# One streaming-encoder layer: another order of the column blocks in the input projection, and one subtraction moved from GpSimd to VectorE

## The chip, the cores and the metric

The kernel runs on one core of a Trainium2 chip. The metric is the device time of one execution in microseconds (us). A core has a matrix engine (TensorE, PE in the profile, with its weight loads as PEld), VectorE (DVE), ScalarE (ACT), GpSimd (POOL) and SyncE (SP); each runs its own queue of instructions in order, and semaphores tie the queues together. SP, POOL and ACT also issue DMA transfers.

## The reference

The layer takes x (2048 tokens of 1024 channels) and 256 memory tokens, all in 32-bit floats. It has three parts: token mixing, cross attention into the memory, and a SwiGLU feed-forward with 2816 channels, each between two RMS norms and added to its input. The change lies in the mixing, which starts with one projection into 2816 columns:

```
u = rms_norm(h, g_mix_pre[l])
z = u @ w_in[l]
qa, ka, va, qh, fh, ih, gh = jnp.split(z, IN_SPLITS, axis=-1)
ya = swa_with_sinks(qa, ka, va, sinks[l])          # sliding-window attention
yh = hgrn2(qh, fh, ih, gh, lb, hgrn_onorm[l])      # gated linear recurrence, 4 heads of 128
y = jnp.concatenate([ya, yh], axis=-1) @ w_out[l]
```

In the recurrence the forget columns become decays. They are summed in chunks of 64 tokens, and the value in the middle of each chunk is subtracted before the exponentials:

```
qf = silu(q) * Dk ** -0.5
f = lb + (1 - lb) * sigmoid(f_logit); kf = 1 - f
b = cumsum(log(f)) within the chunk; b_mid = b[CHUNK // 2 - 1]
A = (qf * exp(b - b_mid)) @ (kf * exp(b_mid - b)).T
```

## The kernel before

**Numbers.** Every operand of a large product is split into a rounded high part and the rest (the low part), and each product is three matmuls, high by high, high by low and low by high (L1098, L1099, L1100). Splitting costs one pass for the high part, on ACT (L962) or POOL (L964), and one DVE pass for the low part (L965).

**Columns.** The 2816 columns of the input projection are 22 columns of 128: 0 to 5 for the attention, 6 to 9 the recurrence's queries, 10 to 13 its forget values, 14 to 17 its inputs i, 18 to 21 its gates g. The projection is computed transposed (columns on partitions, tokens along the free dimension), for the first 1024 tokens and then for the second 1024. The list `ORDER` (L427) gives eleven pairs of columns:

```
    ORDER = [(4, 5), (0, 1), (2, 3)] + [(10 + h, 6 + h) for h in range(4)] + [(c, c + 1) for c in range(14, 22, 2)]
```

**First half** (`in_first`, to about 240 us). Each pair is a block of 256 columns by 1024 tokens. The three attention blocks are computed plainly; the other eight go by a scheme with seven products in place of eight: the weights come in two raw tiles (`sraw`), some are added or subtracted on DVE (`sum`, L1067), each is split (`S`), and each product is 12 matmuls of 128x512 into one of the PSUM banks `psm`. ACT copies finished products away as addends (`part`, L1113), and DVE adds them to a later product (L602) into the block's result tile, `pair`. That last step empties the accumulator, so TensorE's next product in that bank waits for it. Then an activation follows: tanh on ACT (L608) and a scaling on POOL (L610) for a forget column, tanh (L614) and a DVE product (L615) for a query or a gate, nothing for i. TensorE computes the products of block after block; the blocks' follow-up work is emitted between the steps of the next block.

**Decays.** A forget column is followed by `decays` (L695 to L726): logarithm on ACT (L703), which needs the table of its function loaded first, two scans of 128x512 on DVE (L707, printed in the order as SCALAR_TENSOR_TENSOR), a copy of the middle values on POOL (L711, 128x16), the subtraction of the middle value from all 128x1024 (L712), small sums on POOL (L713, L716, L720), two exponentials on ACT (L721, L723) and a DVE pass (L726). Afterwards the query column of the same pair is multiplied by the exponential on DVE (L638).

**Second half.** `in_proj` goes through the same `ORDER` column by column, as 48 matmuls for each 512 tokens, between the steps of the sliding-window attention and the recurrence of the first half, and then between those of the second half's attention. There `decays` gets its two tiles from the pools `x` (three buffers) and `u`. In the second attention loop the same `x` tiles also hold pieces of the output weights `w_out`, which are added and subtracted and stored as `w_s` for a later product of the seven-product kind.

**Order.** A Python program emits all instructions in one stream. A scheduler then moves instructions within each engine's queue by estimated times, with the dependences and the buffers of the pools kept. So a change of `ORDER` moves instructions on every engine.

Of the kernel before, what the change touches and what calls it, by code (L numbers as in the profile page):

```python
# [11 lines left out]
F32 = mybir.dt.float32  # L12
# [3 lines left out]
ALU = mybir.AluOpType  # L16
AX = mybir.AxisListType

P = 128
T = 2048  # L20
D = 1024
# [12 lines left out]
C_KA, C_VA, C_QH, C_FH, C_IH, C_GH = 512, 640, 768, 1280, 1792, 2304  # L34
# [14 lines left out]
class Layer:  # L49
# [374 lines left out]
        self.W = ph.tile([P, 4, P], F32, tag="W", name="W0", bufs=3)  # L424
        nc.gpsimd.memset(self.W, 0.0)

    ORDER = [(4, 5), (0, 1), (2, 3)] + [(10 + h, 6 + h) for h in range(4)] + [(c, c + 1) for c in range(14, 22, 2)]  # L427

    def pair_tile(self):
        self._n += 1  # L430
        return self.st_pool.tile([P, 2, D], F32, tag="pair", name=f"pair_{self._n}", bufs=6)

    def normed(self, x, junk):
        nc = self.nc
        ss = self.small("n_s")
        nc.scalar.activation(junk, x, AF.Square, accum_out=ss)
        r = self.rstd([ss], D, "n")
        nc.vector.scalar_tensor_tensor(x, x, r, self.g_mix, ALU.mult, ALU.mult)

    def in_first(self):  # L440
# [13 lines left out]
        def x_load(q, s):  # L454
            for k in range(4):
                self.load(raw[q, s][:, k, :], I["x_t"][2 * s + q, :, k, :])
# [74 lines left out]
        def parted():  # L531
            for n in (1, 3, 2, 0):
# [5 lines left out]
                with self.behind() if n else contextlib.nullcontext():  # L538
# [7 lines left out]
                  + self.in_block(*p, beside[i], get if i > 6 else (), None if i else lambda: x_load(0, 0))  # L546
                  for i, p in enumerate(self.ORDER)]

# [22 lines left out]
    def in_block(self, ca, cb, beside, get, between):  # L571

        nc, w = self.nc, self.I["w_in"]
        z, bare = [], []

        def load(t, j):
            for i, c in enumerate((ca, cb)):
                if between and i and not j:
                    between()
                self.load(t[:, i, :], w[c, :, j * 512:(j + 1) * 512])  # L580

        def stream(kind):
            for _ in range(2):
                next(iter(get), None)
            return self.streamed(load, 4, kind, tiled=True)

        def out(i, j, a, b):
            if not z:
                z.append(self.pair_tile())
                bare.append(self.r_half is None)  # L590
            c0 = (ca, cb)[i] * P
            sl = slice(j * 512, (j + 1) * 512)
            zs = z[0][:, i, sl]
            if bare[0]:
                nc.scalar.activation(zs, a, AF.Copy)
                return
            if b is None:
                if ca < 6:
                    nc.vector.tensor_tensor(zs, a, self.r_half[:, sl], ALU.mult)
                    return  # L600
            else:
                nc.vector.tensor_tensor(zs, a, b, ALU.add)  # L602
                a = zs
            if C_IH <= c0 < C_GH:
                if b is None:
                    nc.scalar.activation(zs, a, AF.Copy)
            elif C_FH <= c0 < C_IH:
                nc.scalar.activation(zs, a, AF.Tanh, scale=0.5)  # L608
                h = (c0 - C_FH) // P
                nc.gpsimd.tensor_scalar(zs, zs, self.fb[:, h:h + 1], self.fa[:, h:h + 1], ALU.mult, ALU.add)  # L610
            else:
                self._n += 1
                t = self.st_pool.tile([P, 512], F32, tag="part", name=f"th_{self._n}", bufs=self.parts)
                nc.scalar.activation(t, a, AF.Tanh, scale=0.5)  # L614
                nc.vector.scalar_tensor_tensor(zs, t, 1.0, a, ALU.add, ALU.mult)  # L615

        def after():
            def rows(n):
                self._n += 1
                t = self.st_pool.tile([P, D], F32, tag="xr", name=f"xr_{self._n}", bufs=1)  # L620
                with self.behind():
                    self.load(t, self.I["x"][TB + n * P:TB + (n + 1) * P, :])
                return t

            while self.r_bc is None:
                yield
            if bare[0]:
                for i in range(2):
                    with self.behind():
                        nc.gpsimd.tensor_tensor(z[0][:, i, :], z[0][:, i, :], self.r_bc, ALU.mult)  # L630
            t = rows(beside[0]) if beside else None
            c0 = ca * P
            if C_FH <= c0 < C_IH:
                e = self.pair_tile()
                yield from self.decays(0, (c0 - C_FH) // P, z[0][:, 0, :], e[:, 0, :], e[:, 1, :])
                for j in range(2):
                    sl = slice(j * 512, (j + 1) * 512)
                    nc.vector.scalar_tensor_tensor(z[0][:, 1, sl], z[0][:, 1, sl], -0.5 * float(P) ** -0.5,  # L638
                                                   e[:, 0, sl], ALU.mult, ALU.mult)
            for i, c in enumerate((ca, cb)):  # L640
                (self.store if c < 18 else self.store_late)(self.z_d[c * P:(c + 1) * P, 0:TB], z[0][:, i, :])
            for _ in range(1 if C_FH <= c0 < C_IH else 3):
                yield
            for n in beside:
                if n != beside[0]:
                    t = rows(n)
                    for _ in range(3):
                        yield
                ss = self.small("n_s")
                with self.behind():  # L650
                    nc.scalar.activation(t, t, AF.Square, accum_out=ss)
                self.rstd([ss], D, "n", self.r_u[:, NPB + n:NPB + n + 1])
                yield

        return stream, out, after, None

    def in_proj(self, b, u):
        order = [c for p in self.ORDER for c in p]
        e1 = None
        for cols in [order[:2]] + [[c] for c in order[2:]]:  # L660
            e1 = self.in_cols(b, u, cols, e1)
            yield
# [35 lines left out]
    def decays(self, b, h, f, e1, e2):  # L698

        nc = self.nc  # L700
        NCB = TB // 64
        yield
        nc.scalar.activation(e1, f, AF.Ln)  # L703
        yield
        for s in range(TB // 512):
            sl = slice(s * 512, (s + 1) * 512)
            nc.vector.tensor_tensor_scan(e2[:, sl], self.reset.rearrange("p a b -> p (a b)"), e1[:, sl], 0.0,  # L707
                                         ALU.mult, ALU.add)
        b16 = e2.rearrange("p (c t) -> p c t", t=64)
        mid = self.small("d_mid", NCB)  # L710
        nc.gpsimd.tensor_scalar(mid, b16[:, :, 31], 1.0, 1.0, ALU.mult, ALU.mult)  # L711
        nc.gpsimd.tensor_tensor(b16, b16, mid.unsqueeze(2).broadcast_to([P, NCB, 64]), ALU.subtract)  # L712
        nc.gpsimd.tensor_scalar(self.dl[:, h, b * NCB + 1:(b + 1) * NCB + 1], b16[:, :, 63], 1.0, 1.0,  # L713
                                ALU.mult, ALU.mult)
        gs = self.small("d_g", NCB)
        nc.gpsimd.tensor_tensor(gs, mid, self.dl[:, h, b * NCB:(b + 1) * NCB], ALU.add)  # L716
        yield
        g2 = gs.rearrange("p (n c) -> p n c", c=2)
        nc.scalar.activation(self.G1[:, b * NPB:(b + 1) * NPB, h], g2[:, :, 1], AF.Exp)
        nc.gpsimd.tensor_tensor(g2[:, :, 1], g2[:, :, 0], g2[:, :, 1], ALU.add)  # L720
        nc.scalar.activation(e1, e2, AF.Exp)  # L721
        yield
        nc.scalar.activation(e2, e2, AF.Exp, scale=-1.0)  # L723
        nc.scalar.activation(self.G[:, b * NPB:(b + 1) * NPB, h, :], g2, AF.Exp)
        yield
        nc.vector.scalar_tensor_tensor(f, f, 1.0, e2, ALU.subtract, ALU.mult)  # L726
# [1035 lines left out]
```

## Time and profile before

| | before |
|---|---|
| median of 3 runs | 2573.41 us (2573.24 to 2574.53) |
| the profiled execution, its own time | 2571.13 us |
| its span in the trace | 2569.4 us |
| mean granted TensorE clock | 0.995 |
| first half's input projection | to about 240 us |
| second half's projection, with attention and recurrence | about 240 to 740 us |
| cross attention and feed-forward | the rest |

The profile shows one execution; an instruction's row has its start and its duration, and in brackets how long its engine had been idle before it and what ended that idle time. The granted clock is the share of full speed at which TensorE was allowed to run. The times of the stages are read from the lines that run in them.

### The profile page before, as it was taken

What the parts mean: (1) busy time and instruction counts of PE and PEld (TensorE: products, weight loads), DVE (VectorE), ACT (ScalarE), POOL (GpSimd) and SP (SyncE); (2) the same over time, 40 slices, a digit from 0 to 9 for tenths busy, and PEclk for the clock granted to TensorE, in tenths of its full rate; (3) what the DMA queues carried; (4) which work ended last, traced back from release to release, by engine and by line L of the source; (5) the groups of instructions that cost most, each with busy time, mean ns of one, the idle gap of its engine ahead of it and who ended that gap; (6) DMA issues with size and microseconds to landing.
All of it is one profiled execution on the core that took longest, in us unless ns stands there. A gap on an engine that the chain in (4) does not pass through costs nothing.

```text
span 2569.4 us, 34131 instructions
## 1 busy us (share of the span) xinstructions
PE 2517.3 (98%) x12012; PEld 2095.3 (82%) x12012; DVE 1751.8 (68%) x2801; ACT 1254.1 (49%) x2614; POOL 459.4 (18%) x637
## 2 busy tenths in 40 slices
PE   8999999999999999999999999999999999999998
PEld 7777888878997888888788888888888888888886
DVE  6876578877666578697785655575666566664756
ACT  5553366655554565565564333353333334543443
POOL 2341344320322233224210000000000000000022
PEclk9999999999999999999999999999999999999999
DMA  6262645484896896777983542253555434576798
GB/s 238 91 221 100 192 152 171 131 257 157 278 316 226 230 281 206 254 235 198 311 274 121 169 165 77 82 197 124 180 201 192 159 128 142 191 221 185 224 224 210
DMA packets 277835, 495.22 MB, mean 193 GB/s; under 512 B 20897, under 2 KB 135585, under 8 KB 277153
## 3 DMA queue, kind: packets, MB, share of 16 engines
q1 hardware_dynamic: 264128, 443.76, 51.7%
q0 software_dynamic: 11232, 40.90, 8.3%
q10 hardware_dynamic: 2304, 8.39, 0.8%
q8 instruction: 94, 1.54, 0.2%
q14 instruction: 77, 0.62, 0.1%
HBM read 330.45 MB, written 162.53 MB: 192 GB/s over the span
## 4 chain that ended last, share of the span: by engine, by line
PE 81%; DMA 7%; DVE 5%; issue 3%; POOL 2%; ACT 2%; SPq 0%; DVEq 0%; POOLq 0%; ACTq 0%
PE psm L1098 23%; PE psm L1100 22%; PE psm L1099 22%; PE psg L170 2%; PE psg L172 2%; PE psg L171 2%; PE pss L1351 1%; DVE S L965 1%; DMA qd<-z_d 1%; DMA row<-h_d 1%; DMA row<-d_s 1%; DMA kk<-z_d 1%; DMA row<-in_x_dram 1%; DVE T L965 1%; PE pss L811 0%
## 5 line engine op out<-in xcount | busy, mean ns | idle before, releaser
L1098 PE MATMUL psm<-T,S 128*128 128x512 f32 x2744 | 1063.1, 392 | 11.1 <-ACT S L962 4.5
L1100 PE MATMUL psm<-T,S 128*128 128x512 f32 x2744 | 1065.6, 391 | 8.0 <-DVE S L965 7.8
L1099 PE MATMUL psm<-T,S 128*128 128x512 f32 x2744 | 1071.6, 391 | 0.0
L1098 PEld LDWEIGHTS psm<-T,S 128*128 128x128 f32 x2744 | 516.4, 188 | 123.1 <-ACT S L962 6.5
L1100 PEld LDWEIGHTS psm<-T,S 128*128 128x128 f32 x2744 | 516.3, 188 | 120.0 <-DVE S L965 12.2
L1099 PEld LDWEIGHTS psm<-T,S 128*128 128x128 f32 x2744 | 516.4, 188 | 106.4
L962 ACT ACTIVATE S<-sum 128x512 fp32r<-128x512 f32 (+1 forms) x336 | 206.3, 618 | 328.6 <-PE psm L1100 321.8
L965 DVE TENSOR_TENSOR S<-sraw,S 128x512 fp32r<-128x512 f32 (+1 forms) x312 | 213.0, 690 | 214.5 <-ACT S L962 200.1
L965 DVE TENSOR_TENSOR S<-sum,S 128x512 fp32r<-128x512 f32 (+1 forms) x400 | 275.9, 694 | 77.7 <-ACT S L962 59.8
L1113 ACT ACTIVATE part<-psm 128x512 f32<-128x512 f32 x294 | 172.9, 591 | 182.6 <-PE psm L1100 177.3
L962 ACT ACTIVATE S<-sraw 128x512 fp32r<-128x512 f32 (+1 forms) x271 | 165.7, 617 | 159.6 <-PE psm L1100 149.6
L1469 POOL DMA_DIRECT2D row<-y_d x28 | 25.0, 894 | 1072.0 <-DMA sraw<-hid_d 905.3
L1440 ACT ACTIVATE junk<-row 128x512 f32<-128x512 f32 x160 | 99.6, 624 | 100.3 <-DVE row L1462 35.7
L170 PE MATMUL psg<-u,whi 128*128 128x512 f32 x352 | 143.8, 409 | 1.8 <-POOL whi L152 1.8
L965 DVE TENSOR_TENSOR T<-row,T 128x1024 fp32r<-128x1024 f32 x104 | 124.2, 1201 | 30.4 <-ACT T L962 30.2
L172 PE MATMUL psg<-u,wlo 128*128 128x512 f32 x352 | 142.2, 404 | 0.5 <-DVE wlo L153 0.5
L171 PE MATMUL psg<-u,whi 128*128 128x512 f32 x352 | 142.5, 405 | 0.0
L962 ACT ACTIVATE T<-row 128x1024 fp32r<-128x1024 f32 x104 | 105.3, 1023 | 21.9 <-DMA row<-in_w_down_dram 9.4
L1644 DVE TENSOR_TENSOR part<-psm,part 128x512 f32<-128x512 f32 x66 | 45.4, 688 | 65.0 <-PE psm L1100 64.9
L964 POOL TENSOR_SCALAR S<-sum 128x512 fp32r<-128x512 f32 x64 | 48.6, 765 | 218.2 <-PE psm L1100 158.0
L153 DVE TENSOR_TENSOR wlo<-raw,whi 128x1024 fp32r<-128x1024 f32 x54 | 69.3, 1283 | 23.1 <-ACT whi L150 18.4
L1635 DVE TENSOR_TENSOR row<-psm,part 128x512 f32<-128x512 f32 x66 | 45.4, 688 | 55.2 <-PE psm L1100 55.1
(329 smaller groups left out, 3461.2 us busy)
## 6 DMA issues: line engine op xcount, KB each, us to landing
sraw<-in_w_gate_dram SPq DMA_DIRECT2D x44, 512.0 KB, 5.1
sraw<-in_w_up_dram SPq DMA_DIRECT2D x44, 512.0 KB, 4.9
hid_d<-row SPq DMA_DIRECT2D x44, 512.0 KB, 2.7
h_d<-row SPq DMA_DIRECT2D x32, 512.0 KB, 7.0
y_d<-row SPq DMA_DIRECT2D x32, 512.0 KB, 4.0
sraw<-hid_d SPq DMA_DIRECT2D x32, 512.0 KB, 5.4
row<-h_d POOLq DMA_DIRECT2D x30, 512.0 KB, 7.7
row<-y_d POOLq DMA_DIRECT2D x28, 512.0 KB, 7.6
```

Source lines behind the costliest of these rows:

```text
L153: nc.vector.tensor_tensor(lo, raw, f32(hi), ALU.subtract)
L170: nc.tensor.matmul(ps, ah, bh, start=(i == 0), stop=False)
L171: nc.tensor.matmul(ps, ah, bl, start=False, stop=False)
L172: nc.tensor.matmul(ps, al, bh, start=False, stop=(i == n - 1))
L962: self.nc.scalar.activation(hi, raw, AF.Copy)
L964: self.nc.gpsimd.tensor_scalar(hi, raw, 1.0, 1.0, ALU.mult, ALU.mult)
L965: self.nc.vector.tensor_tensor(lo, raw, f32(hi), ALU.subtract)
L1098: nc.tensor.matmul(ps, s[:, 0, k, :], t[:, 0, k, :], start=st, stop=False, **kw)
L1099: nc.tensor.matmul(ps, s[:, 0, k, :], t[:, 1, k, :], start=False, stop=False, **kw)
L1100: nc.tensor.matmul(ps, s[:, 1, k, :], t[:, 0, k, :], start=False, stop=sp, **kw)
L1113: nc.scalar.activation(t, ps, AF.Copy)
L1440: self.nc.scalar.activation(junk, a, AF.Square, scale=float(D) ** -0.5, accum_out=to)
```

## The change

Two things. First, `ORDER` now puts a pair of i or gate columns behind each pair with a forget column, where before the four pairs with forget columns stood in a row: (10, 6), (14, 15), (11, 7), (16, 17), (12, 8), (18, 19), (13, 9), (20, 21). The second half follows the same list. Secondly, the subtraction of the middle value runs on DVE in the first half and stays on POOL in the second. Beside that, the last forget column of the first half gets one of the `g` tiles and the single `xr` tile in place of a `pair` tile for its logarithms and sums.

```
-    ORDER = [(4, 5), (0, 1), (2, 3)] + [(10 + h, 6 + h) for h in range(4)] + [(c, c + 1) for c in range(14, 22, 2)]
+    ORDER = [(4, 5), (0, 1), (2, 3)] + [p for h in range(4) for p in ((10 + h, 6 + h), (14 + 2 * h, 15 + 2 * h))]
...
+    def xr_tile(self):
+        self._n += 1
+        return self.st_pool.tile([P, D], F32, tag="xr", name=f"xr_{self._n}", bufs=1)
...
             if C_FH <= c0 < C_IH:
-                e = self.pair_tile()
-                yield from self.decays(0, (c0 - C_FH) // P, z[0][:, 0, :], e[:, 0, :], e[:, 1, :])
+                h = (c0 - C_FH) // P
+                if h < 3:
+                    e = self.pair_tile()
+                    e1, e2 = e[:, 0, :], e[:, 1, :]
+                else:
+                    e1, e2 = self.gain_tile(), self.xr_tile()
+                yield from self.decays(0, h, z[0][:, 0, :], e1, e2)
...
-        nc.gpsimd.tensor_tensor(b16, b16, mid.unsqueeze(2).broadcast_to([P, NCB, 64]), ALU.subtract)
+        (nc.gpsimd if b else nc.vector).tensor_tensor(b16, b16, mid.unsqueeze(2).broadcast_to([P, NCB, 64]),
+                                                      ALU.subtract)
```

Lines move down in the changed kernel: L602 is L606, L707 is L715, L712 is L720, L721 is L730, L726 is L735, L965 is L974, L1067 is L1076.

The queue of DVE at the decays of column 10, the first forget column, at about 112 us. `pair_853` holds its logarithms and sums, `pair_752` is the result tile of block (10, 6), `pair_914` that of the next block (its row L602 or L606 is an eviction), `S` are split weights and `sum` their combinations. Before:

```order
L965 TENSOR_TENSOR S_940<-sraw_664,S_940 128x512
L707 SCALAR_TENSOR_TENSOR pair_853<-reset,pair_853 128x512 x2
L602 TENSOR_TENSOR pair_914<-psm_945,part_844 128x512
L965 TENSOR_TENSOR S_961<-sraw_825,S_961 128x512
L638 SCALAR_TENSOR_TENSOR pair_752<-pair_752,pair_853 128x512 x2
L965 TENSOR_TENSOR S_986<-sum_984,S_986 128x512
L602 TENSOR_TENSOR pair_914<-psm_854,part_887 128x512
L726 SCALAR_TENSOR_TENSOR pair_752<-pair_752,pair_853 128x1024
```

After:

```order
L974 TENSOR_TENSOR S_935<-sraw_664,S_935 128x512
L715 SCALAR_TENSOR_TENSOR pair_853<-reset,pair_853 128x512 x2
L606 TENSOR_TENSOR pair_914<-psm_940,part_844 128x512
L974 TENSOR_TENSOR S_954<-sraw_825,S_954 128x512
L720 TENSOR_TENSOR pair_853<-pair_853,d_mid_896 128x1024
L974 TENSOR_TENSOR S_977<-sum_975,S_977 128x512
L1076 TENSOR_TENSOR sum_1051<-sraw_825 128x512
L646 SCALAR_TENSOR_TENSOR pair_752<-pair_752,pair_853 128x512 x2
L606 TENSOR_TENSOR pair_914<-psm_854,part_887 128x512
L735 SCALAR_TENSOR_TENSOR pair_752<-pair_752,pair_853 128x1024
```

Behind the scans follow an eviction and a split (`S_961`, now `S_954`) as before. Then the subtraction (L720) comes in, and the product of the query (L638, now L646), which stood ahead of the next split (`S_986`, now `S_977`), stands behind it and a sum. `pair_914` is block (11, 7) before and block (14, 15) after.

The same queue at the decays of column 11, from the scans on. Before, from about 122 us, where `pair_1024` holds the sums and `pair_914` is block (11, 7), and L615 is the query's product:

```order
L707 SCALAR_TENSOR_TENSOR pair_1024<-reset,pair_1024 128x512 x2
L602 TENSOR_TENSOR pair_914<-psm_831,part_867 128x512
L965 TENSOR_TENSOR S_1042<-sum_1040,S_1042 128x512
L965 TENSOR_TENSOR S_1062<-sum_1060,S_1062 128x512
L1067 TENSOR_TENSOR sum_1160<-sraw_994,sraw_997 128x512
L615 SCALAR_TENSOR_TENSOR pair_914<-th_937,pair_914 128x512
L1067 TENSOR_TENSOR sum_1195<-sum_1160,sraw_994 128x512
L965 TENSOR_TENSOR S_1089<-sraw_828,S_1089 128x512
L638 SCALAR_TENSOR_TENSOR pair_914<-pair_914,pair_1024 128x512
L1067 TENSOR_TENSOR sum_1220<-sraw_997,sum_1195 128x512
L726 SCALAR_TENSOR_TENSOR pair_914<-pair_914,pair_1024 128x1024
```

After, where `pair_1182` holds the sums and `pair_1068` is block (11, 7); it comes a whole block later:

```order
L715 SCALAR_TENSOR_TENSOR pair_1182<-reset,pair_1182 128x512 x2
L1076 TENSOR_TENSOR sum_1304<-sraw_1149,sraw_1152 128x512
L720 TENSOR_TENSOR pair_1182<-pair_1182,d_mid_1225 128x1024
L1076 TENSOR_TENSOR sum_1339<-sum_1304,sraw_1149 128x512
L1076 TENSOR_TENSOR sum_1365<-sraw_1152,sum_1339 128x512
L646 SCALAR_TENSOR_TENSOR pair_1068<-pair_1068,pair_1182 128x512
L974 TENSOR_TENSOR S_1264<-sraw_988,S_1264 128x512
L619 SCALAR_TENSOR_TENSOR pair_1068<-th_1137,psm_991 128x512
L974 TENSOR_TENSOR S_1245<-sraw_988,S_1245 128x512
L646 SCALAR_TENSOR_TENSOR pair_1068<-pair_1068,pair_1182 128x512
L735 SCALAR_TENSOR_TENSOR pair_1068<-pair_1068,pair_1182 128x1024
```

Before, an eviction (L602) and two splits stood right behind the scans; now it is one sum, the subtraction, two more sums, the product of the first half of the query (L646), and then the splits.

ACT's queue at the same place. Before:

```order
L608 ACTIVATE pair_914<-pair_914 128x512
L703 ACT_TABLE_LOAD
L703 ACTIVATE pair_1024<-pair_914 128x1024
L962 ACTIVATE S_1042<-sum_1040 128x512
L614 ACT_TABLE_LOAD
L614 ACTIVATE th_937<-pair_914 128x512
L962 ACTIVATE S_1089<-sraw_828 128x512
L721 ACTIVATE pair_1024<-pair_1024 128x1024
```

After:

```order
L612 ACTIVATE pair_1068<-pair_1068 128x512
L711 ACT_TABLE_LOAD
L711 ACTIVATE pair_1182<-pair_1068 128x1024
L659 ACTIVATE xr_1013,n_s_1080<-xr_1013 128x1024
L730 ACT_TABLE_LOAD
L730 ACTIVATE pair_1182<-pair_1182 128x1024
L618 ACTIVATE th_1137<-psm_991 128x512
```

The exponential (L730) now has a table load of its own right ahead of it, since the query's tanh (L618, L614 before) moved behind it.

SP's queue in the second attention loop: `x` are pieces of `w_out`, `w_s` the stored combinations, `z_d` stored columns, `qd`, `kr`, `vr` the attention's loads, `raw` weights. Before:

```order
L75 DMA x_5148<-in_w_out_dram 128x2x512
L78 DMA w_s<-x_4934 128x1024
L75 DMA x_5150<-in_w_out_dram 64x2x512 x2
L75 DMA qq_6404<-z_d 128x4x128
L75 DMA qq_6571<-z_d 128x4x128
L75 DMA x_5361<-in_w_out_dram 64x2x512 x2
L78 DMA y_d<-ys_4818 128x512
L78 DMA w_s<-x_5148 128x1024
L75 DMA x_5572<-in_w_out_dram 128x2x512
L78 DMA z_d<-z_5094 128x1024
L75 DMA qd_1_5161<-z_d 64x4x128 x2
L75 DMA kr_5378<-z_d 64x2x256 x2
```

After:

```order
L75 DMA x_5122<-in_w_out_dram 128x2x512
L75 DMA x_5124<-in_w_out_dram 64x2x512 x2
L75 DMA raw_6271<-in_w_in_dram 128x1024
L75 DMA qd_1_5350<-z_d 64x4x128
L78 DMA y_d<-ys_4991 128x512
L75 DMA qd_1_5350<-z_d 64x4x128
L75 DMA kr_5568<-z_d 64x2x256 x2
L78 DMA z_d<-z_5049 128x1024
L78 DMA w_s<-x_5122 128x1024
L75 DMA x_5339<-in_w_out_dram 64x2x512 x2
L75 DMA qd_0_5556<-z_d 64x4x128 x2
L75 DMA raw_6337<-in_w_in_dram 128x1024
```

Three loads into `x` tiles stand here where four stood, and one store of a combination where there were two; two loads of weights and more of the attention's loads lie between them.

More of the change, by code (lines that the diff above doesn't have):

```diff
@@ L618, in rows @@
             def rows(n):
-                self._n += 1
-                t = self.st_pool.tile([P, D], F32, tag="xr", name=f"xr_{self._n}", bufs=1)
+                t = self.xr_tile()
                 with self.behind():
@@ L638, in after @@
                     nc.vector.scalar_tensor_tensor(z[0][:, 1, sl], z[0][:, 1, sl], -0.5 * float(P) ** -0.5,
-                                                   e[:, 0, sl], ALU.mult, ALU.mult)
+                                                   e1[:, sl], ALU.mult, ALU.mult)
             for i, c in enumerate((ca, cb)):
```

## Prediction

> **What bounds it now.** I read the page first, then the stretches, the waits of TensorE and the timeline around each wait.
>
> ```profile
> PE 2517.3 (98%) x12012; PEld 2095.3 (82%) x12012; DVE 1751.8 (68%) x2801; ACT 1254.1 (49%) x2614; POOL 459.4 (18%) x637
> ```
>
> TensorE is busy for 98% of the span, so whatever this change can bring is idle time of TensorE or time at a lower clock. The stretches show where that is (columns: span, busy time and count of PE, PEld, DVE, ACT, POOL, then the granted clock, DMA share, GB/s):
>
> ```profile
> 100.00:150.00 50.00, 46.10 (x190) 36.20 (x188) 39.79 (x48) 32.43 (x47) 24.91 (x29) 0.97 0.42 155
> 150.00:200.00 50.00, 45.49 (x183) 35.84 (x183) 35.68 (x49) 25.35 (x43) 18.19 (x26) 0.93 0.52 183
> 200.00:250.00 50.00, 49.12 (x214) 39.37 (x213) 32.21 (x49) 15.25 (x26) 6.65 (x12) 1.00 0.22 81
> 112.00:115.40 3.40, 2.49 (x12) 1.74 (x11) 2.82 (x3) 2.18 (x3) 3.32 (x4) 1.00 0.00 0
> 115.40:118.80 3.40, 3.40 (x17) 2.77 (x16) 3.40 (x5) 1.68 (x3) 2.66 (x4) 1.00 0.28 116
> 122.90:126.30 3.40, 0.67 (x3) 0.58 (x4) 3.40 (x4) 2.21 (x4) 1.14 (x2) 1.00 0.29 87
> 126.30:129.70 3.40, 3.40 (x10) 2.65 (x9) 3.40 (x5) 2.67 (x5) 2.33 (x4) 0.50 0.01 2
> 150.20:153.60 3.40, 1.21 (x4) 0.73 (x5) 3.40 (x6) 2.88 (x7) 1.93 (x4) 1.00 0.00 0
> 153.60:157.00 3.40, 3.40 (x10) 2.63 (x9) 3.01 (x5) 1.09 (x4) 1.94 (x2) 0.50 0.42 143
> 174.10:177.50 3.40, 1.42 (x5) 0.89 (x6) 3.40 (x6) 2.87 (x8) 1.80 (x4) 1.00 0.00 0
> 177.50:180.90 3.40, 3.40 (x10) 2.61 (x9) 3.40 (x5) 0.90 (x2) 1.94 (x2) 0.50 0.45 154
> 546.20:549.60 3.40, 0.96 (x7) 0.82 (x7) 2.43 (x8) 1.22 (x3) 0.02 (x1) 0.99 1.06 331
> 549.60:553.00 3.40, 3.40 (x10) 2.62 (x9) 3.27 (x9) 2.64 (x8) 1.39 (x3) 0.50 1.02 378
> ```
>
> From 200 to 250 us, TensorE starts 214 matmuls in 50 us, one every 0.234 us. The four forget blocks fall into 100 to 200 us, where it starts 190 and 183: 24 + 31 are missing, 12.9 us. The waits of TensorE in that stretch name them (us in total, times, longest):
>
> ```profile
> PE psm L1100 <- DVE S L965: 5.0, 4, 1.9
> PE psm L1098 <- DVE pair L602: 2.8, 1, 2.8
> PE psm L1098 <- ACT S L962: 0.7, 2, 0.4
> ```
>
> That is 8.5 us of waits. The rest is the clock: after each of the three wide gaps the clock stands at 0.50 for 3.4 us, which loses 1.7 us each time, 5.1 us in all. Together 13.6 us, close to the 12.9 us from the count. A stretch of 3.4 us with 2.49 us of work (0.91 idle) kept the clock; stretches with 1.42 us or less of work (1.98 idle or more) lost it. So a gap costs its width, and 1.7 us more from somewhere between 0.91 and 1.98 us of idling on.
>
> **The subtraction.** Four times 128x1024 leave POOL in the first half; the price on DVE is that of the nearest row, L726, another pass with two operands in SBUF over 128x1024:
>
> ```profile
> L712 POOL TENSOR_TENSOR pair<-pair,d_mid 128x1024 f32<-128x1024 f32 x4 | 7.6, 1905 | 0.3
> L726 DVE SCALAR_TENSOR_TENSOR pair<-pair,pair 128x1024 f32<-128x1024 f32 x4 | 4.9, 1214 | 0.0
> ...
> 112.25 1.90 POOL L712 TENSOR_TENSOR pair<-pair,d_mid 128x1024 f32<-128x1024 f32 x1
> 112.37 2.33 DVE L965 TENSOR_TENSOR S<-sraw,S 128x512 fp32r<-128x512 f32 x1
> 114.76 0.50 PE L1100 MATMUL psm<-T,S 128*128 128x512 f32 x1 [0.91 <-DVE S L965]
> ```
>
> While POOL subtracts, the DVE pass beside it takes 2.33 us where such a pass of 128x512 takes 0.68 (below). So POOL's subtraction already cost DVE 1.65 us; on DVE it costs 1.21. DVE's time falls by 0.4 us per chain, and the S split that used to hang now ends 1.65 us earlier. The upper bound for the new pass is POOL's own 1.9 us. [...]
>
> The new wait is DVE's for POOL's middle value (L711, ahead of nothing but a small chain on POOL), and behind it on DVE stand the splits that TensorE needs next.
>
> **Column 10's chain.** By the orders above, the S split behind the scans now runs before the subtraction, at about 113.05, so the 0.91 us go. The widest gap comes from column 11's chain, which started while column 10's block was hardly done:
>
> ```profile
> 122.66 2.34 DVE L707 TENSOR_TENSOR_SCAN pair<-reset,pair 128x512 f32<-128x512 f32 x2 [2.03 <-ACT pair L703]
> 124.91 0.67 DVE L602 TENSOR_TENSOR pair<-psm,part 128x512 f32<-128x512 f32 x1
> 125.64 0.50 PE L1098 MATMUL psm<-T,S 128*128 128x512 f32 x1 [2.77 <-DVE pair L602]
> ```
>
> An accumulator could not be emptied until the scans were through. In the changed order the next block is (14, 15), and no scan stands ahead of that eviction. The subtraction ends at 114.3, the table load and exponential that follow it (2.3, prices below) at 116.6, and the eviction is the sixth pass of 0.68 after that, with L726's 1.21 among them: 121.9 us. TensorE, without the 0.91, arrives at 122.0. 0.9 + 2.8 us of waits and one clock loss go; what is late next there is this same eviction, by tenths.
>
> **Columns 11, 12 and 13.** Their chains still stand in the DVE queue ahead of a split that TensorE needs. Today:
>
> ```profile
> 146.86 2.35 DVE L965 TENSOR_TENSOR S<-sum,S 128x512 fp32r<-128x512 f32 x1
> ...
> 151.99 1.09 DVE L965 TENSOR_TENSOR S<-sraw,S 128x512 fp32r<-128x512 f32 x1
> 153.13 0.50 PE L1100 MATMUL psm<-T,S 128*128 128x512 f32 x1 [1.92 <-DVE S L965]
> 147.03 1.28 ACT L614 ACT_TABLE_LOAD   x1 [2.31 <-DVE pair L602]
> ```
>
> The split that TensorE waits for is one of the passes piled up behind the scans. The last row, of ACT, matters too: a table load can wait with the instruction that it serves. The prices in the stretch (mean ns):
>
> ```profile
> L602 DVE TENSOR_TENSOR pair<-psm,part 128x512 f32<-128x512 f32 x13 | 8.8, 679 | 2.1 <-PE psm L1100 2.1
> L608 ACT ACTIVATE pair<-pair 128x512 f32<-128x512 f32 x7 | 4.4, 631 | 3.0 <-DVE pair L602 3.0
> L703 ACT ACT_TABLE_LOAD x4 | 5.1, 1283 | 0.1
> L703 ACT ACTIVATE pair<-pair 128x1024 f32<-128x1024 f32 x4 | 4.2, 1060 | 0.0
> L721 ACT ACTIVATE pair<-pair 128x1024 f32<-128x1024 f32 x4 | 4.2, 1051 | 1.1 <-POOL pair L712 1.1
> ```
>
> For column 11, count from the end of the product that completes the forget column. Eviction 0.15 + 0.68, tanh 0.63, table load 1.28, logarithm 1.06, scans 2.34: 6.1. Then in the queue shown above one sum 0.68 and the subtraction 1.21: 8.0. ACT's exponential now has its table load right ahead of it, both behind the subtraction: 1.28 + 1.05, 10.4 (the two sums hide under it). Then four passes of 0.68: 13.1. TensorE needs that last split 48 matmuls after the same point, at 11.2: a gap of 1.9, as wide as today's, because the table load eats what the subtraction gives. For column 12 the input rows' square and three passes of 0.68 hold the scans back to 7.0; scans, sum, gate, subtraction and two splits (2.34 + 4 x 0.68 + 1.21) end at 13.3 (12.9 with overlapping starts) against 49 matmuls and four transposes, 11.8: 1.1 to 1.5. For column 13 scans end at 6.1, then one eviction, the subtraction and six passes of 0.68: 12.1 against 11.2: 0.9. Sum with 0.2 for the port each: 1.9 + 1.3 + 0.9 + 0.6 = 4.7 us. Of clock losses I expect 1.2 instead of three (0.6, 0.35 and 0.25 by the width of the gaps): 2.0 us. If a load of weights comes late for the sum ahead of the subtraction, add 1 to 3 us; if the table load does not wait, column 11's gap falls to 0.6.
>
> **The rest of the first half.** Evictions, gates and the copies for the second half keep their numbers; the last block ends with the same two splits ahead of the projection, so the wait at its end stays. POOL's two late stores stand behind blocks without decays, as today. Forget column 13 uses the gain tile and the row tile; the last reader of each is a block or more ahead, so I take nothing; were one late, it would hold the scans by that much.
>
> **The second half.** The column order moves there too; its subtraction stays on POOL. The chain of column 12 goes from the first attention loop to the second. Waits of TensorE from 260 to 720 us:
>
> ```profile
> PE pss L811 <- DVE vst L763: 2.4, 1, 2.4
> PE pst L858 <- ACT atz L860: 1.7, 1, 1.7
> PE psh L821 <- DVE ptl L816: 1.2, 2, 1.1
> PE pss L811 <- DVE w_mn L782: 0.9, 1, 0.9
> ```
>
> The first one, with its clock loss (546 and 549 us above) 4.1 us, comes where DVE waits for w_out pieces that are loaded close together. In the new SP order these pieces stand further apart, but share three x tiles with two chains instead of one. That may remove 4.1 us or add as much; I take nothing.
>
> Sum: waits 8.5 to 4.7, clock 5.1 to 2.0: 13.6 - 6.7 = 6.9 us saved. The profiled execution took 2571.13 us, 1.7 more than its span; the median is 2573.41. Taken off the median: 2566.5.
>
> **Rivals.**
> [...]
> *All goes.* The three gaps fall under 0.9: 2573.4 - 13.6 = 2559.8, if they vanish. Against it: each sum above still ends late.
> *Slower, by the second half.* In the second attention loop the DVE queue waits for w_out pieces with attention splits behind it; column 12's and 13's chains hold an x tile, so SP's loads wait and those behind them too. Each such stall at 4.1 us; it decides from three on (12.3 - 6.9 = 5.4 over before), and with four it is 2582.9. For it: DVE's late release there today; against it: one such stall today with the loads crowded.
> *The clock does not hang on these gaps.* [...] All gaps here are under 2.8 us, yet each from 1.9 us on is followed by half clock, so the trace speaks against it. If the losses stayed for another reason, only waits would go: 2573.4 - 3.8 = 2569.6.
>
> **How the numbers follow.** My forecast 0.53, stalls stay 0.24, all goes 0.09, slower 0.10, clock unmoved 0.04. My forecast's own range is 2562 to 2571: no clock loss and narrower gaps at one end, three losses at the other. 2560 to 2575 takes in the second rival and most of the others, and leaves out the slower one and the far end of "all goes". A measurement of this kernel can tell about 0.2%, 5.15 us, so faster means under 2568.3: 0.7 of my forecast, all of "all goes", a little of the first rival, 0.49. Slower means above 2578.6: 0.10. The same: 0.41.
>
> **What would show it.** Right: between 100 and 200 us (now shorter) TensorE's waits sum to 4 to 5 us, none on L602 (now L606); one or two stretches at 0.50; no DVE split above 1.2 us beside a subtraction; column 11's exponential starts a table load after the subtraction. Wrong: three clock losses there; a DVE wait on sraw ahead of the subtraction; more than one wait above 2 us between 500 and 650 us.

## The result, and the profile after

The changed kernel takes 2567.43 us (median of 17 runs, 2561.8 to 2572.75) against 2573.07 us (17 runs, 2568.71 to 2577.43) of the kernel before. The ratio is 0.9981, with a 95% interval of 0.9973 to 0.9988: 3 to 7 us faster, at best guess 4.9, against a forecast of 6.9 us and 2566.5 us.

The profiled execution took 2568.33 us, its span is 2566.6 us. TensorE is as busy as before:

```profile
PE 2516.8 (98%) x12012; PEld 2097.4 (82%) x12012; DVE 1754.7 (68%) x2805; ACT 1254.0 (49%) x2614; POOL 457.5 (18%) x633
```

The stretches of the first half, with the columns as in the prediction. The four forget blocks lie further apart now. Against 214 matmuls in 50 us, 21 are missing in the first stretch, around column 11, 3 in the second and 18 in the last. In the last stretch TensorE is idle for 4.1 us: column 13's split (0.8), a late eviction behind it (0.9), and the wait for the second half's first weights (1.8 and 0.5), which now falls into it.

```profile
100.00:150.00 50.00, 45.54 (x193) 36.38 (x192) 36.24 (x51) 27.85 (x45) 17.45 (x26) 0.97 0.45 164
150.00:200.00 50.00, 49.97 (x211) 40.23 (x211) 32.18 (x45) 23.70 (x40) 14.39 (x23) 0.97 0.57 197
200.00:250.00 50.00, 45.92 (x196) 36.22 (x196) 42.84 (x60) 27.13 (x40) 13.15 (x18) 0.99 0.33 114
```

TensorE's waits from 100 to 240 us (us in total, times, longest):

```profile
PE psm L1107 <- ACT part L1122: 3.8, 1, 3.8
PE psm L1109 <- DVE S L974: 0.8, 1, 0.8
PE psm L1107 <- DVE pair L606: 0.7, 1, 0.7
```

Column 10's eviction is 0.7 us late, column 13's split 0.8, column 12 causes no wait. One wide gap is left, at column 11. The prediction had a gap of 1.9 us there, for a split on DVE; this one is wider and has another cause. ACT's timeline shows it, with TensorE's next matmul:

```profile
144.93 1.28 ACT L730 ACT_TABLE_LOAD   x1 [2.92 <-DVE pair L720]
146.22 1.06 ACT L730 ACTIVATE pair<-pair 128x1024 f32<-128x1024 f32 x1
147.19 0.58 ACT L618 ACTIVATE th<-psm 128x512 f32<-128x512 f32 x1
147.66 0.59 ACT L1122 ACTIVATE part<-psm 128x512 f32<-128x512 f32 x1
...
148.31 0.79 PE L1107 MATMUL psm<-T,S 128*128 128x512 f32 x1 [3.78 <-ACT part L1122]
```

ACT stood idle for 2.92 us until DVE's subtraction was done, then loaded the table, then computed the exponential. Only behind these came the copy that empties an accumulator. The clock stood at 0.50 from 146.65 to 153.48 us, of which TensorE worked 5.2 us, a further loss of 2.6.

How much each part of the program took is read between three matmuls that every version has: the first of the seven-product blocks (the one that waits 0.69 us for a copy), the first of the second half (L170), and the first of the next `psm` stage, in cross attention. By the second of these the first half's projection lasted to 254 us before, not to about 240. Before:

```profile
85.35 0.50 PE L1098 MATMUL psm<-T,S 128*128 128x512 f32 x1 [0.69 <-ACT part L1113]
254.47 0.50 PE L170 MATMUL psg<-u,whi 128*128 128x512 f32 x1 [1.84 <-POOL whi L152]
789.27 0.50 PE L1098 MATMUL psm<-T,S 128*128 128x512 f32 x1 [1.88 <-ACT S L962]
```

After:

```profile
85.04 0.50 PE L1107 MATMUL psm<-T,S 128*128 128x512 f32 x1 [0.69 <-ACT part L1122]
247.68 0.50 PE L170 MATMUL psg<-u,whi 128*128 128x512 f32 x1 [1.84 <-POOL whi L152]
782.83 0.50 PE L1107 MATMUL psm<-T,S 128*128 128x512 f32 x1 [1.89 <-ACT S L971]
```

First half 169.12 to 162.64 us, 6.5 saved; second half 534.80 to 535.15, 0.35 lost. The rest, up to the end of the span, took 1780.1 and 1783.8 us in these two executions; in the nine profiled executions of this study it lies between 1780 and 1788 us, in no order that follows the edits to the first 790 us. That is why one trace's span says less than its first 790 us.

### The profile page after: what moved, and what is told of

The parts are those of the page before. It is cut to its first block, busy times and chain, and to the rows that moved or that the text cites. A ratio compares the mean times of both kernels' runs of the same rounds, so it can differ in the third digit from the quotient of the medians.

```text
span 2566.6 us, 34125 instructions
## 1 busy us (share of the span) xinstructions
PE 2516.8 (98%) x12012; PEld 2097.4 (82%) x12012; DVE 1754.7 (68%) x2805; ACT 1254.0 (49%) x2614; POOL 457.5 (18%) x633
## 4 chain that ended last, share of the span: by engine, by line
PE 82%; DMA 6%; issue 5%; DVE 4%; ACT 2%; POOL 1%; SPq 0%; POOLq 0%; DVEq 0%; ACTq 0%
PE psm L1107 21%; PE psm L1109 21%; PE psm L1108 21%; PE psg L172 3%; PE psg L170 3%; PE psg L171 3%; PE pss L1360 1%; DMA row<-in_x_dram 1%; DMA row<-h_d 1%; DMA row<-y_d 1%; DVE S L974 1%; DMA y_d<-row 1%; ACT junk L1449 1%; PE pss L820 0%; PE pst L820 0%
## 5 line engine op out<-in xcount | busy, mean ns | idle before, releaser
L974 DVE TENSOR_TENSOR S<-sraw,S 128x512 fp32r<-128x512 f32 (+1 forms) x312 | 211.2, 684 | 214.3 <-ACT S L971 199.8
L974 DVE TENSOR_TENSOR S<-sum,S 128x512 fp32r<-128x512 f32 (+1 forms) x400 | 272.8, 686 | 82.0 <-ACT S L971 65.0
L170 PE MATMUL psg<-u,whi 128*128 128x512 f32 x352 | 143.7, 408 | 3.9 <-DVE z L693 2.1
L974 DVE TENSOR_TENSOR T<-row,T 128x1024 fp32r<-128x1024 f32 x104 | 123.4, 1194 | 30.8 <-ACT T L971 30.5
```

The lines of the kernel that those rows point to most:

```text
L170: nc.tensor.matmul(ps, ah, bh, start=(i == 0), stop=False)
L974: self.nc.vector.tensor_tensor(lo, raw, f32(hi), ALU.subtract)
```

## The experiments

The two parts of the change were first separated, then the second half, then the gap at column 11. Medians, ratios to the kernel before with their intervals, and the first and second half of the profiled execution as defined above. Each ratio is to runs of the kernel before in the same series: 17 with a median of 2573.07 for the changed kernel, 27 with 2572.43 for the next four versions, 15 with 2571.27 for the last three. Versions of different series are therefore compared by their ratios:

| version | median us (runs) | ratio, 95% interval | first half us | second half us |
|---|---|---|---|---|
| before | 2573.07 (17) | | 169.12 | 534.80 |
| changed kernel | 2567.43 (17) | 0.9981 [0.9973, 0.9988] | 162.64 | 535.15 |
| order alone | 2569.02 (11) | 0.9984 [0.9976, 0.9993] | 163.87 | 536.50 |
| subtraction alone | 2574.25 (11) | 1.0008 [0.9999, 1.0017] | 172.52 | 533.78 |
| changed, second half in old order | 2565.43 (11) | 0.9978 [0.9967, 0.9988] | 161.86 | 535.39 |
| changed, exponential behind copies | 2562.55 (5) | 0.9959 [0.9945, 0.9973] | 155.87 | 534.88 |
| that, column 11's small exponential too, subtraction on POOL | 2562.26 (11) | 0.9973 [0.9964, 0.9982] | 156.60 | 534.02 |
| its twin, subtraction on DVE | 2558.46 (5) | 0.9962 [0.9949, 0.9974] | 155.80 | 536.85 |
| the twin, second half in old order | 2561.62 (5) | 0.9962 [0.9949, 0.9974] | 155.86 | 532.99 |

### The order alone

```
-        (nc.gpsimd if b else nc.vector).tensor_tensor(b16, b16, mid.unsqueeze(2).broadcast_to([P, NCB, 64]), ALU.subtract)
+        nc.gpsimd.tensor_tensor(b16, b16, mid.unsqueeze(2).broadcast_to([P, NCB, 64]), ALU.subtract)
```

> The new column order in both halves, the subtraction back on POOL in the first half. Queue theory: what TensorE loses at a forget column is set by what stands ahead of a split or of an accumulator's release in the queues of DVE and ACT. Here the query's tanh has its table load ahead of the exponential, so no load waits for the subtraction, but both exponentials (1.06 us each), a square (1.06) and the tanh stand ahead of column 11's copy of an addend, and the exponentials wait for POOL's 1.9 us: the gap at column 11, 3.78 us in the changed kernel, is 5 to 6 us, and the split beside POOL's subtraction at column 10 takes 2.3 us again and costs 0.5 to 0.9. About 2570 to 2572 us, 2.5 to 4.5 above the changed kernel. Rival, spacing alone: a block without decays behind each forget column gives the whole gain and the engine of the subtraction does not matter: within 1.5 us of the changed kernel, 2566 to 2569. Second rival, the subtraction gives the gain: the time of the kernel before, 2573.

2569.02 us, and TensorE's waits from 100 to 236 us are these:

```profile
PE psm L1106 <- ACT part L1121: 5.2, 2, 4.9
PE psm L1108 <- DVE S L973: 0.9, 1, 0.9
```

This version keeps the other tiles of the last forget column, which no run separates from the order. The gaps are where the queues said: 4.9 us at column 11 (5 to 6 expected), 0.9 at column 10. In time the spacing alone is the closer rival: the first half is 1.2 us longer than in the changed kernel where 2.5 was the least that I expected, and the two ratios cannot be told apart. The new order carries the gain. The passes beside POOL's subtraction do hang, the split at column 10 and a sum at column 11 that takes 0.7 us elsewhere:

```profile
111.04 2.33 DVE L973 TENSOR_TENSOR S<-sraw,S 128x512 fp32r<-128x512 f32 x1
...
142.19 2.39 DVE L1075 TENSOR_TENSOR sum<-sraw,sraw 128x512 f32<-128x512 f32 x1
```

With a block between two chains, DVE has room for that, but for the 0.9 us at column 10.

### The subtraction alone

```
-        nc.gpsimd.tensor_tensor(b16, b16, mid.unsqueeze(2).broadcast_to([P, NCB, 64]), ALU.subtract)
+        (nc.gpsimd if b else nc.vector).tensor_tensor(b16, b16, mid.unsqueeze(2).broadcast_to([P, NCB, 64]), ALU.subtract)
```

This is an edit of the kernel before; all its decays keep their `pair` tiles.

> The old column order in both halves, only the subtraction on DVE in the first half. Queue theory: column 10's 0.91 goes, since no split runs beside POOL any more; column 11's 2.77 us with its 1.7 of clock stays, since the scans still stand ahead of that eviction; the 1.92 at columns 12 and 13 become 1 to 2, since the new 1.21 replaces the stretch of 1.65 of one split. 1 to 3.5 us saved: 2569.5 to 2572. Rival, the subtraction gives the whole gain: 2567.5 or less. Rival, it costs: 1.21 us more ahead of the splits at three columns with the clock kept low: 2575 to 2577.

2574.25 us, 0.1% slower at best guess, and the interval just reaches no change. The first half is 3.4 us longer than before. Of the three expectations the third, that it costs, comes nearest. Waits from 100 to 236 us:

```profile
PE psm L1101 <- DVE S L966: 3.8, 2, 1.9
PE psm L1099 <- DVE pair L602: 3.3, 1, 3.3
PE psm L1099 <- ACT S L963: 2.8, 2, 1.4
PE psm L1099 <- ACT part L1114: 1.2, 1, 1.2
```

Column 10's 0.91 went, as expected. But column 11 lost 3.3 us in place of 2.8 and 1.2 more for a copy, and columns 12 and 13 kept their 1.9 us and each got 1.4 more, for a split on ACT. ACT and DVE at column 12 show why for that column:

```profile
149.59 1.06 ACT L724 ACTIVATE pair<-pair 128x1024 f32<-128x1024 f32 x1
150.55 0.61 ACT L963 ACTIVATE S<-sraw 128x512 fp32r<-128x512 f32 x1
...
150.95 1.62 DVE L727 SCALAR_TENSOR_TENSOR pair<-pair,pair 128x1024 f32<-128x1024 f32 x1
152.50 0.68 DVE L1068 TENSOR_TENSOR sum<-sum,sraw 128x512 f32<-128x512 f32 x1
153.11 0.68 DVE L966 TENSOR_TENSOR S<-sraw,S 128x512 fp32r<-128x512 f32 x1
```

In the kernel before, the split stands ahead of the second exponential on ACT, and its low part (151.99 us) ahead of the 128x1024 pass on DVE:

```profile
149.81 0.61 ACT L962 ACTIVATE S<-sraw 128x512 fp32r<-128x512 f32 x1
...
151.06 1.04 ACT L723 ACTIVATE pair<-pair 128x1024 f32<-128x1024 f32 x1
...
153.60 1.21 DVE L726 SCALAR_TENSOR_TENSOR pair<-pair,pair 128x1024 f32<-128x1024 f32 x1
```

With the faster subtraction the end of the chain comes earlier in the queues, now ahead of the split that TensorE waits for, and nobody needs that end early.

### The second half

```
-        order = [c for p in self.ORDER for c in p]
+        order = [c for p in [(4, 5), (0, 1), (2, 3)] + [(10 + h, 6 + h) for h in range(4)]
+                 + [(c, c + 1) for c in range(14, 22, 2)] for c in p]
```

> The changed first half, but the second half goes through its columns in the old order. The trace of the changed kernel reaches the second half 6.8 us earlier than before, and the feed on from cross attention 6.4 us earlier, so the second half's order took back 0.3 us net. If its order is as neutral as that: within 1.5 us of the changed kernel. If the new waits there (4.4, 2.2 and 2.1 us, where before it was 2.4, 1.7 and 1.1) come from the new order and cost more than the trace of one execution shows: 2 to 4 us below the changed kernel. If the new order removed a stall that depends on it (the 2.4 us behind the w_out pieces): 2 to 4 us above it.

2565.43 us: 2.0 us below the changed kernel by the medians, 0.8 by the ratios, and within the two 95% intervals the same. But the stalls are others. The changed kernel's waits from 500 to 660 us begin so:

```profile
PE psg L879 <- ACT atz L869: 4.4, 1, 4.4
PE pst L884 <- DMA v<-z_d: 2.2, 1, 2.2
PE psg L170 <- DVE z L693: 2.1, 1, 2.1
```

With the second half in the old order they begin with 1.7 and 1.5 us:

```profile
PE pst L867 <- ACT atz L869: 1.7, 1, 1.7
PE pss L820 <- DVE vst L772: 1.5, 1, 1.5
```

The 4.4 us are the mechanism of the "slower" rival, on ACT in place of DVE: a step of the recurrence stands behind a split that waits for a piece of `w_out`.

```profile
633.93 1.06 ACT L971 ACTIVATE T<-z 128x1024 fp32r<-128x1024 f32 x1 [3.07 <-DMA z<-in_w_out_dram]
```

So the new order removed one group of stalls and brought another of about the same price. Over all nine traces the second half took 533.0 to 535.4 us in the old order (four traces) and 534.0 to 536.9 in the new one (five).

### The exponential behind the copies

```
-        nc.scalar.activation(e1, e2, AF.Exp)
+        with contextlib.nullcontext() if b or h != 1 else self.tc.issue_after(self.last[mybir.EngineType.Activation]):
+            nc.scalar.activation(e1, e2, AF.Exp)
```

> The changed kernel, and column 11's exponential of the first half issued on ACT behind the tanh and the two copies of addends that it stood in front of; nothing else is moved by hand. Queue theory: the 3.78 us for the copy and the half clock behind it (2.5 us of the next twelve matmuls) were the table load and the exponential waiting for the subtraction: both go, 5 to 6.3 us, 2561 to 2562.5, with no TensorE wait over 1 us between 120 and 240 us. Rival, late splits: DVE's splits would have been late there too, by 1.3 to 1.9 us as forecast, so 2 to 4.5 us are saved and a wait on DVE S takes the place: 2563 to 2565.5. Rival, moved on: the exponential now delays the product of the query or the next block by as much, no change, 2566 to 2569.

2562.55 us; by the ratios 5.7 us below the changed kernel, with intervals that touch. The first half is 6.8 us shorter, and the waits from 100 to 236 us are short:

```profile
PE psm L1110 <- DVE S L975: 0.8, 1, 0.8
PE psm L1108 <- DVE pair L606: 0.7, 1, 0.7
PE psm L1108 <- ACT part L1123: 0.5, 1, 0.5
```

ACT's queue at column 11 is now this:

```profile
141.50 1.28 ACT L618 ACT_TABLE_LOAD   x1
...
144.14 0.59 ACT L1123 ACTIVATE part<-psm 128x512 f32<-128x512 f32 x1
...
148.39 1.05 ACT L731 ACTIVATE pair<-pair 128x1024 f32<-128x1024 f32 x1
```

The 3.78 us and the half clock behind them were the exponential ahead of the copy, with its table load, which now stands ahead of the tanh and runs while ACT has nothing to do. That is shown: only the exponential was moved by hand, and the copy now ends 9.2 us behind the start of the forget column's eviction, where it ended 12.5 behind it. Whether DVE's splits would have been late at column 11, as forecast, it does not show, since the scheduler moved them too: they now stand ahead of the query's product and end at 147.96 us, where in the changed kernel they ended at 149.81. (1.1 of the 6.8 us come from a shorter wait for the second half's first weights, and 0.9 of that comes back just behind the boundary, in the wait for their low part.)

### With that out of the way, which engine subtracts

```
-        nc.scalar.activation(self.G1[:, b * NPB:(b + 1) * NPB, h], g2[:, :, 1], AF.Exp)
+        with contextlib.nullcontext() if b or h != 1 else self.tc.issue_after(self.last[mybir.EngineType.Activation]):
+            nc.scalar.activation(self.G1[:, b * NPB:(b + 1) * NPB, h], g2[:, :, 1], AF.Exp)
```

This comes on top of the edit before. One version has the subtraction on POOL, its twin on DVE, the third is the twin with the second half in the old order.

> The new column order, the subtraction on POOL in the first half as before, and column 11's exponentials of the first half (the small one too) issued on ACT behind the two tanh and the copies they stood in front of. With the order alone, column 11's copy was 4.93 us late and the half clock behind it two stretches long. Theory, the engine is neutral: the loss at column 11 came only from exponentials ahead of copies, wherever the subtraction runs; all of it goes here, 7 to 8 us against the order alone, and what stays of POOL's subtraction is the 0.9 us of column 10's split beside it. The second half begins within 1.5 us of the moment at which it does in the twin with DVE, and the time is 2561.5 to 2564. Rival, DVE is what makes room: beside POOL's subtraction DVE's passes take 2.3 to 2.4 us and hold the splits at columns 11 to 13; the second half begins 2 to 5 us later than in the twin: 2564.5 to 2568. Rival, DVE costs: the twin with DVE loses more by POOL's own work being held up beside it, the second half begins 1.5 us or more earlier here: below 2561.

> The twin of the run before with the subtraction on DVE, as in the changed kernel; against the earlier version, which moved only the large exponential, the small one moves too. Theory: no further loss at column 11, the second half begins at 240 to 241.5 us, and the time is that of the earlier version, 2562.55 us, within 1.5 us: 2561 to 2564. If the 7 us there were an accident of the trace: 2565 to 2568, as the changed kernel.

> The run before, and the second half in the old column order. With the changed order TensorE waited in the second half 4.4 us for a step of ACT that stood behind a load of w_out pieces, with two stretches of half clock; in the old order it waited 2.4 us behind DVE in another place. Theory, a trade of stalls: both orders lose the same there, within 1.5 us of the run before. Rival, the old order is the better one: 2 to 4 us below it, 2558 to 2560.5, with no wait on ACT over 2 us between 600 and 650 us.

2562.26, 2558.46 and 2561.62 us; the ratios of the three have overlapping intervals, and medians of five runs that spread over 6 to 8 us, as the last two are, say no more than the ratios do (2558.46 lies below the 2561 to 2564 that I expected, and 2561.62 more than 1.5 above it). The first half of the twins is 156.60 with POOL and 155.80 with DVE: 0.8 us for DVE, inside the 1.5 that I called neutral. With POOL column 10 waits 0.9 for its split and column 11's copy is still 1.7 us late:

```profile
PE psm L1108 <- ACT part L1123: 2.0, 2, 1.7
PE psm L1110 <- DVE S L975: 0.9, 1, 0.9
```

The second half's order is again neutral: 0.9962 both times. In this pair of traces the old order's second half is 3.9 us shorter, and no wait on ACT above 1.6 us is left between 600 and 650 us, as the rival asked; but over all nine traces the means are 534.2 us in the old order and 535.5 in the new, and a difference of that size is not resolved here. The twins on DVE, like the version before them, are 0.4% faster than the kernel before and some 0.2% faster than the changed kernel; their intervals end at 0.9974, where that of the changed kernel begins at 0.9973.

## Why the prediction came out as it did

**Right: what the gain is.** The waits and half clock of the forget blocks fell, and the second half gave nothing net. Forecast 6.9 us saved; the trace has 6.5 in the first half and 0.35 back in the second; the ratio gives 3 to 7, with the forecast at its upper end.

**Right: column 10 and column 13.** "Late by tenths" for the eviction was 0.68, "0.9" for column 13 was 0.83.

**Wrong step: column 11.** The prediction counted DVE's queue to a split at 13.1 us and let TensorE need it at 11.2. In the trace DVE's two splits there ended 12.9 and 14.1 us after the forget column's eviction began at 135.71, so as a count of DVE's queue it was near. But I followed only DVE. On ACT, right behind the exponential whose table load I had priced, stood the copy that empties an accumulator, and TensorE needed that first; behind so wide a gap the late splits did not show. 1.9 us and 0.6 of a clock loss (1.0 us) were forecast; 3.78 and 2.6 us were lost.

**Wrong step: column 12.** 1.1 to 1.5 us and 0.35 of a clock loss were forecast, none came, in the order alone as well. DVE's queue was as long as counted. The forget column's product ended about 0.15 us ahead of its eviction at 180.99, at 180.84 us, and then came these:

```profile
187.85 2.33 DVE L715 TENSOR_TENSOR_SCAN pair<-reset,pair 128x512 f32<-128x512 f32 x2
192.43 1.28 DVE L974 TENSOR_TENSOR S<-sraw,S 128x512 fp32r<-128x512 f32 x2
193.17 0.40 PE L1107 MATMUL psm<-T,S 128*128 128x512 f32 x1
```

The scans began 7.0 us behind the product, as forecast, and the two splits ended 12.3 and 12.9 behind it, the second as forecast. But TensorE, without a wait, began the product that the sum had put at 11.8 only 12.3 behind it, and only the third of each three matmuls reads the low part of the weights. The step that failed is the moment at which TensorE needs the split: it was set half a microsecond and more too early.

**Wrong term: the subtraction's credit.** I took 0.4 us of DVE time per chain, and a split that no longer runs beside POOL and ends 1.65 us earlier, as a gain. By single traces the subtraction's move is worth 0.8 to 1.2 us in the new order, and in the old order it costs 3.4. The first is hardly more than the 0.8 us by which the first halves of the changed kernel and of the version with the second half in the old order differ, with the same instructions in the same order on DVE, ACT and POOL. The cost of the pass was right: 1.21, 1.22, 1.22 and 1.46 us in the four chains. No run shows the 0.2 us that the sum adds three times for a port: three of the four passes took the 1.21 that was priced, within 0.01, and the last 0.25 more. What I left out is that a chain that ends sooner puts its own tail ahead of splits.

Column 11 lost 3.5 us more than forecast (6.4 against 2.9), column 12 about 2 less, so the sum came out better than its terms: that is luck. In all, 5.3 us of waits and 2.6 of clock were left where 4.7 and 2.0 were forecast.

**The rivals.** "The stalls stay", with the remaining gaps as wide as before (1.92 us) and half clock behind each, holds for one column of three. "All goes" did not happen, and the exponential behind the copies shows what stood in its way. "Slower, by the second half" had the right mechanism and the wrong count: one stall of 4.4 us with two half-clock stretches, two of about 2, and the old ones gone. My own sign for being wrong, more than one wait above 2 us between 500 and 650 us, did show, and the net was still near zero, since it did not count what left. Of the signs for being right, one failed by little: a wait of 0.7 us is on L606, where none was to be. The waits sum to 4.5 us between 100 and 200 us and to 5.3 with column 13's, which comes later now, where I asked for 4 to 5. "The clock does not hang on these gaps" fell: half clock followed the wide gap and no other gap of the forget columns.

## What to carry to other kernels

Follow a moved instruction's wait on its own engine to the end of the queue: what stood behind column 11's exponential cost more than anything on the engine that the change was about. Making a chain faster off the critical path can cost time when its tail then stands ahead of work that is on the path (3.4 us of the first half in one trace here; the whole kernel's 0.1% was not resolved). Give such a tail a place behind that work, which here was worth about as much as the whole change. And spacing the chains so that one has drained before the next begins was worth most of this change's gain (5.2 of 6.5 us in the first half).

## What was not expected of the hardware

The prediction took the half clock as a matter of a gap's width, from somewhere between 0.91 and 1.98 us on. The traces show something sharper: the clock changes on a fixed grid of 3.41 us (in the kernel before, half clock begins at 126.31, 153.61 and 177.50 us, eight and seven times 3.413 us apart, and each of the 732 stretches of that grid in its trace has a mean clock of 1.00 or 0.50), and a stretch of that grid at full clock in which TensorE was idle for 1.72 us or more, about half of it, was followed by one at half clock in 34 of 35 cases. Two gaps of the same wait, the first of 2.07 us in the changed kernel, cut in two by a border of the grid (0.90 and 1.16 us idle):

```profile
600.65:604.06 3.41, 2.51 (x14) 1.75 (x12) 3.35 (x6) 2.51 (x5) 0.00 (x0) 1.00 0.97 276
604.06:607.47 3.41, 2.25 (x10) 1.83 (x11) 3.41 (x9) 0.00 (x0) 0.00 (x0) 1.00 1.17 276
```

The second of 2.08 us with the exponential behind the copies, 1.94 us of it in one stretch:

```profile
596.09:599.50 3.41, 1.47 (x6) 1.24 (x7) 3.41 (x8) 0.50 (x1) 0.00 (x0) 1.00 1.14 254
599.50:602.91 3.41, 3.41 (x9) 2.64 (x8) 3.41 (x8) 0.00 (x0) 1.34 (x1) 0.50 1.03 399
```

And the narrowest pair, 1.71 us idle in the last version and 1.72 in the order alone:

```profile
762.34:765.75 3.41, 1.70 (x8) 1.06 (x6) 0.00 (x0) 0.00 (x0) 0.00 (x0) 1.00 1.02 410
765.75:769.16 3.41, 2.55 (x10) 1.83 (x11) 1.23 (x1) 2.03 (x3) 0.00 (x0) 1.00 0.78 219
...
246.69:250.10 3.41, 1.69 (x6) 1.12 (x7) 2.47 (x4) 3.41 (x5) 3.41 (x5) 1.00 0.89 281
250.10:253.51 3.41, 3.41 (x10) 2.65 (x9) 3.41 (x3) 0.43 (x1) 3.41 (x3) 0.50 1.05 312
```

Of the stretches at full clock between 90 and 800 us of the nine traces that were idle for more than 1.2 us, all 16 with up to 1.71 us kept the clock, and 34 of the 35 with 1.72 or more lost it (the other one had 1.89). Beyond 800 us the edge is less sharp: the kernel before kept the clock behind a stretch with 1.73 us idle (at 1273.18 us), and the changed kernel lost it behind one with 1.74 (at 1269.63). A stretch that was itself at half clock needed less to be followed by another: 1.66 us idle was enough behind column 11's gap, and 0.80 in the last version at 632.64 us, while 0.46 in the version with the second half in the old order at 639.78 was not. Where the grid lies differs from one execution to the next: it has a border at 88.62 us in the changed kernel's trace and at 86.82 in that with the second half in the old order, 1.80 us apart. So a gap of about 2 us cost its width or 1.7 us more by where the borders fell, as the gaps of 2.07 and 2.08 us above show. The same 3.78 us at column 11 brought two stretches at half clock in the changed kernel's trace and one in that with the second half in the old order, whose first half is 0.8 us shorter. That this makes up the spread of some 10 us between runs of one kernel is likely, but was not tried.
